# Convolution in the mixing stage: VectorE's own first tap first, the bank of diagonal products added last

## The chip, the cores and the metric

The kernel runs on one NeuronCore of a Trainium2 chip. The metric is device time in microseconds (us) of one execution, inputs and weights in HBM, result in HBM. The engines are named as in the profile: PE (TensorE matmul), PEld (its weight loads, which overlap), DVE (VectorE), ACT (ScalarE), POOL (GpSimd), SP (SyncE, here only a DMA queue).

## The reference

Two transformer blocks in a row on 256 tokens of 1024 channels. The first has two layers (l = 0, 1); layer 0 treats the tokens and a context of 256 more rows, layer 1 the tokens alone. A layer's mixing stage is one product with `w_in` and four mixers side by side, attention, a Fourier mixer, a convolution and a pooling mixer, each 256 channels wide:

```python
def conv_module(a, dw_w, dw_b, ln_g, ln_b, w_pw):
    glu = a[..., :W_CONV] * jax.nn.sigmoid(a[..., W_CONV:])
    y = lax.conv_general_dilated(glu, dw_w[:, None, :], window_strides=(1,),
        padding=[(CONV_WIDTH // 2, CONV_WIDTH // 2)], ...
        feature_group_count=W_CONV) + dw_b          # 31 taps, each channel by itself
    y = jax.nn.silu(layer_norm(y, ln_g, ln_b))
    return y @ w_pw
...
    mix = jnp.concatenate([attn, four, conv, pool], axis=-1) @ w_o
    x = x + gate1 * mix
    xn = rms_norm(x, g2) * (1 + scale2) + shift2
    return x + gate2 * swiglu(xn, w_fi, w_fo)
```

The gates, shifts and scales are products of a conditioning vector with `w_mod` (1024 x 6144 for each layer), one vector for the tokens and one for the context. The second block (dilated attention, a spatial gating unit, a gated feed-forward net) stands behind all this and is not touched.

## The kernel before

Channels lie on the 128 partitions, tokens along the free dimension: 512 columns in layer 0 (context and tokens), 256 in layer 1. fp32 precision comes from splitting each operand in a high and a low part and three matmuls (`mm3`, L273 to L275; L289 to L291 with tokens on the partitions). Weights arrive in halves of 128x1024 over SP's queue into `raw`; ACT casts the high part `wh` (L243), DVE subtracts the low part `wl` (L245), four buffers of each. A half is split when the one that held its buffers has been read for the last time.

In a mixing stage PE computes in this order: the convolution's inputs (`p_c`), q (`p_q`), k and v (`p_kv`), the Fourier input (`p_f`) and the pooling input (`p_p`). In between lie the works of the mixers. Each mixer is a generator that is spawned and runs in steps; a `yield` is the time it lets pass by a planner's clock, and `tick` moves that clock on for the matmuls. So the text is written in an interleaved order, and a scheduler with a timeline model of its own then sets the final order of instructions on PE, DVE, ACT and POOL; SP's queue keeps the written one.

The convolution works on two halves f = 0, 1 of 128 channels. `glu` (L636 on DVE) writes GP, the padded input. Of the 31 taps the first NPE = 8 are done by PE: `conv_diag` (on ACT, ahead) writes 8 diagonal matrices of the tap weights into a tile `cdg`, and `conv_pe` (L578) accumulates 8 fp32 matmuls of them with shifted views of GP in one PSUM bank `p_cv`. The trace has each of these as two records. The other 23 taps are DVE's in `conv_taps`: one instruction that copies bank plus bias into Y (L586), then 23 that add GP times a tap weight to Y (L588). Both halves run as `cv0` and `cv1` beside each other. The `cdg` tiles take two of the four buffers of tag `wm`, the `p_cv` banks two of four small PSUM buffers (`psm`) that the softmax scores `p_s` (L689), the transposes `p_qt` (L675) and the norms use too.

Behind both halves wait two things. `conv_ln` normalises Y (L604 to L620) and multiplies it with `w_pw` (`p_pw`, L627). In layer 0, `mod_bg` also starts then: for every 128 rows of a part of `w_mod`, POOL copies a column of `snap` (one column of the finished Y, L590) into a `wm` tile (L397), which orders the transfer behind it; the transfer of 512 KB is issued by ACT's queue (L398), and DVE forms two products with sums (L402 for the context, L404 for the tokens). Of each pair of tiles the layer's residual update (L891) needs the gate, and the next stage's first `nt` (L339) the norm's scale. `p_fy` is the Fourier mixer's second product, folded by DVE into U (L775, L776); `p_fa` (L755) its first; `p_pl` (L809) the pooling product, behind POOL's chain of sums S (L793 to L804) on the copied `p_p` (UP).

Of the kernel before, what the change touches and what calls it, by code (L numbers as in the profile page):

```python
# [28 lines left out]
OP = mybir.AluOpType  # L29
# [4 lines left out]
T = 256  # L34
NF = 22
EPS = 1e-6
TAPS = 31
# [10 lines left out]
NPE = 8  # L48
# [67 lines left out]
class Flow:  # L116
# [6 lines left out]
    def spawn(self, gen, delay=0.0):  # L123
        t = {"gen": gen, "done": False}
        self.n += 1
        heapq.heappush(self.q, (self.now + delay, self.n, t))
        return t
# [11 lines left out]
    def tick(self, c):  # L139
        self.now += c  # L140
        self._run()
# [13 lines left out]
def tile_kernel(ctx, tc, xin, pk_d, rows_d, lc_d, bc_d, wmod0, wmod, win, wout, wfi, wfo, wsm, win2, wproj, wout2,  # L155
                wgu, wdn, wst, pos, out, dump=None):
    nc = tc.nc
    V, S, G, PE, SP = nc.vector, nc.scalar, nc.gpsimd, nc.tensor, nc.sync
# [12 lines left out]
    def psm(name="psm"):  # L171
        return psum.tile([128, 512], F32, tag="sm", name=name)


    pk = cpool.tile([128, PK_W], F32, name="pk")
# [17 lines left out]
    def P(name, i=0, n=1):  # L193
        return pk[:, PK[name] + i:PK[name] + i + n]
# [40 lines left out]
    def split_to(i):  # L235
        while ld["split"] < min(i, len(halves)):
            j = ld["split"]
            dma_to(j + 1)
            n = halves[j][1]
            raw = ld["raw"].pop(j)  # L240
            h = ring.tile([128, 1024], F32R, tag="wh", name="wh", bufs=WB)
            lo = ring.tile([128, 1024], F32R, tag="wl", name="wl", bufs=WB)
            S.copy(h[:, :n], raw[:, :n])  # L243
            every = SPL.get(halves[j][2], 0) or (1 if j in SPH else 0)
            (G if every and j % every == 0 else V).tensor_tensor(lo[:, :n], raw[:, :n], h[:, :n].bitcast(F32),  # L245
                                                                 op=OP.subtract)
            ld["hl"][j] = (h, lo)
            ld["split"] += 1
            dma_to(j + 1 + RAW)
# [9 lines left out]
    def done(n, c, i=None):  # L259

        for j in (where[n, c] if i is None else [where[n, c][i]]):
            ld["done"].add(j)
        while ld["low"] in ld["done"]:
            ld["low"] += 1
        split_to(ld["low"] + WB)
# [254 lines left out]
    for l in range(2):  # L520
        streams = (0, 1) if l == 0 else (0,)
        ns = len(streams)
        N = 256 * ns
        cs = slice(0, N)
        with ExitStack() as mctx:
# [3 lines left out]
            GP = mp.tile([128, 2, ns, GW], F32, name="GP")  # L529
# [8 lines left out]
            Y = mp.tile([128, 2, N], F32, name="Y")  # L538
# [25 lines left out]
            cps = {}  # L564

            def conv_diag(f):

                w = lpool.tile([128, D], F32, tag="wm", name="cdg", bufs=WMB)
                for j in range(NPE):
                    S.activation(w[:, 128 * j:128 * j + 128], ident, AF.Copy,  # L570
                                 scale=pk[:, PK[f"dw_{l}"] + f * TAPS + j:PK[f"dw_{l}"] + f * TAPS + j + 1])
                return w

            def conv_pe(f, w):

                cps[f] = psm("p_cv")
                for j in range(NPE):
                    PE.matmul(cps[f][:, :N].rearrange("p (s t) -> p s t", t=T), w[:, 128 * j:128 * j + 128],  # L578
                              GP[:, f, :, j:j + T], start=j == 0, stop=j == NPE - 1)
                    tick(0.0017 * N)  # L580

            def conv_taps(f, delay):
                y = Y[:, f].rearrange("p (s t) -> p s t", t=T)
                dw = PK[f"dw_{l}"] + f * TAPS
                per = 0.35 * ns
                V.tensor_scalar(Y[:, f], cps[f][:, :N], P(f"db_{l}", f), None, op0=OP.add)  # L586
                for j in range(NPE, TAPS):
                    V.scalar_tensor_tensor(y, GP[:, f, :, j:j + T], pk[:, dw + j:dw + j + 1], y, op0=OP.mult, op1=OP.add)  # L588
                    yield per + delay
                G.tensor_copy(snap, Y[:, f, 0:1])  # L590
                pace[0] = snap

# [223 lines left out]
            cdg = [conv_diag(f) for f in range(2)]  # L816
# [8 lines left out]
            else:  # L825
                for f in range(2):
# [6 lines left out]
                            fm(ps4[2 + m][:, :N], n_, 1, 128 * m, cs)  # L833
                    glu(f, ps4[2 * f], ps4[2 * f + 1])
                    done(n_, f)
            for f in range(2):
                conv_pe(f, cdg[f])
            cv0 = spawn(conv_taps(0, CVD))
            cv1 = spawn(conv_taps(1, CVD), 0.5)
            cv = spawn(conv_ln(cv0, cv1))  # L840
            if l == 0:
# [10 lines left out]
            for s in ((1, 0) if l == 0 else (0, 1)):  # L852
# [6 lines left out]
                    S.copy(VT[:, 2 * (1 - s) + i], p[:, 128:256])  # L859
                preps[s] = spawn(qk_prep(s), 0.4)  # L860
            done(n_, 3)
            at = []
            if l == 0:
                at.append(spawn(attention(1, [preps[1]])))
# [77 lines left out]
        with ExitStack() as fctx:  # L942
# [64 lines left out]
            else:  # L1007
# [5 lines left out]
                for m in range(22):  # L1013
# [4 lines left out]
                    if m == 0:  # L1018
# [11 lines left out]
                                           op1=OP.mult)  # L1030
# [4 lines left out]
                for m in range(8):  # L1035
                    p = pmm("p_dn")
                    for part in range(2):
# [5 lines left out]
                                           op0=OP.mult, op1=OP.subtract)  # L1043
# [9 lines left out]
    with ExitStack() as bctx:  # L1053
# [238 lines left out]
        for c in range(4):  # L1292
            for b in range(2):
                m = 2 * c + b
                ps2 = []
                for hf in (1, 0):
                    p = pmm("p_pr")
                    for k in range(4):
# [11 lines left out]
                                       op1=OP.subtract)  # L1310
# [3 lines left out]
        for m in range(8):  # L1314
# [8 lines left out]
            elif m >= 4:  # L1323
# [5 lines left out]
                                   op0=OP.mult, op1=OP.subtract)  # L1329
# [5 lines left out]
    with ExitStack() as fctx:  # L1335
# [44 lines left out]
        for q, (m0, m1) in enumerate(OUT):  # L1380
            V.tensor_tensor(OT[:, m0:m1], OT[:, m0:m1], res[1][:, None, :].to_broadcast([128, m1 - m0, 256]),
                            op=OP.mult)
# [103 lines left out]
```

## Time and profile before

| | us |
|---|---|
| median of three runs | 1396.38 |
| the three runs | 1396.1, 1396.38, 1402.08 |
| profiled execution | 1395.62 |
| its span, first to last instruction | 1393.4 |
| PE busy in the span | 1339.7 (96%) |
| DVE busy | 932.3 (67%) |
| ACT busy | 617.5 (44%) |
| POOL busy | 287.9 (21%) |

The mean granted TensorE clock is 0.983 of full speed. The shares are averages over stages of different kinds: the feed-forward nets and the second block keep PE full; layer 0's mixing stage lies at about 60 to 262 us of the span and layer 1's at about 620 to 720 us. The tables of stretches, waits and instructions from which the prediction is made are in the section on rows below.

### The profile page before, as it was taken

What the parts mean: (1) busy time and instruction counts of PE and PEld (TensorE: products, weight loads), DVE (VectorE), ACT (ScalarE), POOL (GpSimd) and SP (SyncE); (2) the same over time, 40 slices, a digit from 0 to 9 for tenths busy, and PEclk for the clock granted to TensorE, in tenths of its full rate; (3) what the DMA queues carried; (4) which work ended last, traced back from release to release, by engine and by line L of the source; (5) the groups of instructions that cost most, each with busy time, mean ns of one, the idle gap of its engine ahead of it and who ended that gap; (6) DMA issues with size and microseconds to landing.
All of it is one profiled execution on the core that took longest, in us unless ns stands there. A gap on an engine that the chain in (4) does not pass through costs nothing.

```text
span 1393.4 us, 23072 instructions
## 1 busy us (share of the span) xinstructions
PE 1339.7 (96%) x9000; PEld 1193.2 (86%) x9000; DVE 932.3 (67%) x1597; ACT 617.5 (44%) x1030; POOL 287.9 (21%) x302
## 2 busy tenths in 40 slices
PE   6799889999999999999899999999999999999997
PEld 2578558888888888889689999999899999999997
DVE  4969999899885333349757666666665567755553
ACT  5623452523214232334555554455665444544452
POOL 3524535233340000121520000120100002322211
PEclk9799989999999999999999999999999999999998
DMA  8322443477895222343225555665325335555463
GB/s 321 136 92 79 166 154 134 152 272 232 278 323 179 91 91 63 104 137 107 78 83 189 183 182 156 187 242 191 122 98 175 122 125 179 181 182 181 153 196 106
DMA packets 66477, 223.77 MB, mean 161 GB/s; under 512 B 7488, under 2 KB 8640, under 8 KB 66368
## 3 DMA queue, kind: packets, MB, share of 16 engines
q1 hardware_dynamic: 53824, 178.16, 38.3%
q10 hardware_dynamic: 12080, 42.50, 9.0%
q0 software_dynamic: 464, 1.64, 0.3%
q8 instruction: 70, 1.15, 0.3%
q14 instruction: 39, 0.32, 0.1%
HBM read 221.22 MB, written 1.05 MB: 160 GB/s over the span
## 4 chain that ended last, share of the span: by engine, by line
PE 84%; DVE 9%; issue 2%; DMA 2%; POOL 1%; ACT 1%; SPq 0%; DVEq 0%; POOLq 0%; ACTq 0%
PE p_dn L273 6%; PE p_dn L275 6%; PE p_dn L274 6%; PE p_ua L273 4%; PE p_ua L274 4%; PE p_ug L273 4%; PE p_ug L275 4%; PE p_ug L274 4%; PE p_ua L275 4%; DVE wm L404 2%; DVE jg L402 2%; PE p_bq L289 2%; PE p_bq L290 2%; PE p_bq L291 2%; PE p_ga L275 2%
## 5 line engine op out<-in xcount | busy, mean ns | idle before, releaser
L245 DVE TENSOR_TENSOR wl<-raw,wh 128x1024 fp32r<-128x1024 f32 (+2 forms) x340 | 390.5, 1151 | 277.7 <-ACT wh L243 275.7
L243 ACT CAST wh<-raw 128x1024 fp32r<-128x1024 f32 (+1 forms) x344 | 331.6, 972 | 310.0 <-PE p_ug L274 89.2
L275 PE MATMUL p_dn<-HH,wl 128*128 128x256 f32 (+1 forms) x550 | 171.9, 313 | 0.5 <-DVE wl L245 0.5
L273 PE MATMUL p_dn<-HH,wh 128*128 128x256 f32 (+1 forms) x550 | 172.0, 313 | 0.0
L274 PE MATMUL p_dn<-HL,wh 128*128 128x256 f32 (+1 forms) x550 | 171.9, 312 | 0.0
L315 POOL TENSOR_TENSOR ss<-ss,sq 128x256 f32<-128x256 f32 (+1 forms) x43 | 49.8, 1158 | 422.2 <-ACT sq L314 284.7
L273 PE MATMUL p_ug<-AH,wh 128*128 128x258 f32 (+2 forms) x368 | 121.9, 332 | 0.6 <-DVE XC L891 0.6
L273 PE MATMUL p_ua<-AH,wh 128*128 128x258 f32 (+2 forms) x368 | 122.0, 333 | 0.4 <-ACT usg L950 0.3
L275 PE MATMUL p_ug<-AH,wl 128*128 128x258 f32 (+2 forms) x368 | 122.0, 332 | 0.0
L274 PE MATMUL p_ug<-AL,wh 128*128 128x258 f32 (+2 forms) x368 | 121.9, 331 | 0.0
L274 PE MATMUL p_ua<-AL,wh 128*128 128x258 f32 (+2 forms) x368 | 121.9, 331 | 0.0
L275 PE MATMUL p_ua<-AH,wl 128*128 128x258 f32 (+2 forms) x368 | 121.7, 331 | 0.0
L275 PEld LDWEIGHTS p_dn<-HH,wl 128*128 128x128 f32 x550 | 104.4, 190 | 6.7 <-DVE wl L245 0.7
L273 PEld LDWEIGHTS p_dn<-HH,wh 128*128 128x128 f32 x550 | 104.4, 190 | 6.1 <-ACT wh L243 0.2
L274 PEld LDWEIGHTS p_dn<-HL,wh 128*128 128x128 f32 x550 | 104.4, 190 | 6.1
L404 DVE SCALAR_TENSOR_TENSOR wm<-wm,scb 128x1024 f32<-128x1024 f32 x80 | 100.9, 1265 | 11.2 <-DMA wm<-in_wmod 10.4
L273 PEld LDWEIGHTS p_ug<-AH,wh 128*128 128x128 f32 x368 | 69.3, 188 | 8.1 <-DVE XC L891 0.8
L273 PEld LDWEIGHTS p_ua<-AH,wh 128*128 128x128 f32 x368 | 69.2, 188 | 7.7 <-ACT usg L950 0.5
L274 PEld LDWEIGHTS p_ua<-AL,wh 128*128 128x128 f32 x368 | 69.4, 189 | 7.3 <-DVE AL L341 0.2
L275 PEld LDWEIGHTS p_ua<-AH,wl 128*128 128x128 f32 x368 | 69.4, 189 | 7.1
L274 PEld LDWEIGHTS p_ug<-AL,wh 128*128 128x128 f32 x368 | 69.5, 189 | 6.9
L275 PEld LDWEIGHTS p_ug<-AH,wl 128*128 128x128 f32 x368 | 69.4, 189 | 6.9
(375 smaller groups left out, 3415.5 us busy)
## 6 DMA issues: line engine op xcount, KB each, us to landing
raw<-in_wfi SPq DMA_DIRECT2D x88, 512.0 KB, 4.0
raw<-in_win SPq DMA_DIRECT2D x84, 512.0 KB, 4.0
wm<-in_wmod ACTq DMA_DIRECT2D x80, 512.0 KB, 4.4
raw<-in_wgu SPq DMA_DIRECT2D x44, 512.0 KB, 3.8
raw<-in_wout SPq DMA_DIRECT2D x24, 512.0 KB, 3.6
raw<-in_wfo SPq DMA_DIRECT2D x32, 384.0 KB, 3.1
raw<-in_wfo SPq DMA_DIRECT2D x32, 320.0 KB, 3.3
raw<-in_wdn SPq DMA_DIRECT2D x16, 384.0 KB, 3.1
```

The lines of the kernel that those rows point to most:

```text
L243: S.copy(h[:, :n], raw[:, :n])
L245: (G if every and j % every == 0 else V).tensor_tensor(lo[:, :n], raw[:, :n], h[:, :n].bitcast(F32), op=OP.subtract)
L273: PE.matmul(ps, w[0], a[0], start=first, stop=False, **kw)
L274: PE.matmul(ps, w[0], a[1], start=False, stop=False, **kw)
L275: PE.matmul(ps, w[1], a[0], start=False, stop=last, **kw)
L289: PE.matmul(ps, a[0], w[0], start=k == 0, stop=False)
L290: PE.matmul(ps, a[0], w[1], start=False, stop=False)
L291: PE.matmul(ps, a[1], w[0], start=False, stop=k == KT - 1)
L315: (eng or G).tensor_tensor(ss[0][:, cs], ss[0][:, cs], sq[:, :n], op=OP.add)
L402: V.scalar_tensor_tensor(jg, w, 1.0, scb[:, 1], op0=OP.mult, op1=OP.mult, accum_out=modv[:, l, part, 1, k:k + 1])
L404: V.scalar_tensor_tensor(w, w, 1.0, scb[:, 0], op0=OP.mult, op1=OP.mult, accum_out=modv[:, l, part, 0, k:k + 1])
```

## The change

`conv_taps` no longer begins with the bank. The first instruction multiplies GP by DVE's first tap weight and adds the bias (L586, a tensor_scalar from SBUF), 22 taps follow (L590 of the new text), then the generator waits until the bank exists and adds it (L594). `conv_pe` for both halves moves from ahead of `cv0` to behind `done(n_, 3)`, the end of k and v in the written text. Lines behind the loop have numbers larger by 6 in the new text (L590 `snap` becomes L596, `glu` L642).

```diff
--- before.py
+++ after.py
@@ -583,10 +583,16 @@
                 y = Y[:, f].rearrange("p (s t) -> p s t", t=T)
                 dw = PK[f"dw_{l}"] + f * TAPS
                 per = 0.35 * ns
-                V.tensor_scalar(Y[:, f], cps[f][:, :N], P(f"db_{l}", f), None, op0=OP.add)
-                for j in range(NPE, TAPS):
+                V.tensor_scalar(y, GP[:, f, :, NPE:NPE + T], pk[:, dw + NPE:dw + NPE + 1], P(f"db_{l}", f), op0=OP.mult,
+                                op1=OP.add)
+                yield per + delay
+                for j in range(NPE + 1, TAPS):
                     V.scalar_tensor_tensor(y, GP[:, f, :, j:j + T], pk[:, dw + j:dw + j + 1], y, op0=OP.mult, op1=OP.add)
                     yield per + delay
+                while f not in cps:
+                    yield 0.3
+                V.tensor_tensor(Y[:, f], cps[f][:, :N], Y[:, f], op=OP.add)
+                yield per
                 G.tensor_copy(snap, Y[:, f, 0:1])
                 pace[0] = snap
 
@@ -833,8 +839,6 @@
                             fm(ps4[2 + m][:, :N], n_, 1, 128 * m, cs)
                     glu(f, ps4[2 * f], ps4[2 * f + 1])
                     done(n_, f)
-            for f in range(2):
-                conv_pe(f, cdg[f])
             cv0 = spawn(conv_taps(0, CVD))
             cv1 = spawn(conv_taps(1, CVD), 0.5)
             cv = spawn(conv_ln(cv0, cv1))
@@ -859,6 +863,8 @@
                     S.copy(VT[:, 2 * (1 - s) + i], p[:, 128:256])
                 preps[s] = spawn(qk_prep(s), 0.4)
             done(n_, 3)
+            for f in range(2):
+                conv_pe(f, cdg[f])
             at = []
             if l == 0:
                 at.append(spawn(attention(1, [preps[1]])))
```

Where the scheduler puts the instructions can be read from the built programs. PE, layer 0, around q: the two banks as they stood (-), between matmuls of q.

```order
 L290 MATMUL p_q<-wl,AH 128x256
 L291 MATMUL p_q<-wh,AL 128x256
-L578 MATMUL p_cv<-GP,cdg 128x512 x8
 L289 MATMUL p_q<-wh,AH 128x256
 L290 MATMUL p_q<-wl,AH 128x256
 L291 MATMUL p_q<-wh,AL 128x256
-L578 MATMUL p_cv<-GP,cdg 128x512 x8
 L289 MATMUL p_q<-wh,AH 128x256
```

Both are gone from there. PE, layer 0, at the end of `p_f`: the first bank as it stands now (+). The `p_qt` are transposes of the context's q and k.

```order
 L275 MATMUL p_f<-AH,wl 128x512
 L273 MATMUL p_f<-AH,wh 128x512
+L681 MATMUL p_qt<-ident,qt_781 128x128 x3
+L578 MATMUL p_cv<-GP,cdg 128x512
+L681 MATMUL p_qt<-ident,qt_815 128x128 x3
+L578 MATMUL p_cv<-GP,cdg 128x512 x7
 L274 MATMUL p_f<-AL,wh 128x512
-L675 MATMUL p_qt<-ident,qt_801 128x128 x3
-L675 MATMUL p_qt<-ident,qt_835 128x128 x3
 L275 MATMUL p_f<-AH,wl 128x512
 L273 MATMUL p_p<-AH,wh 128x512
```

The first bank is behind q, k, v and nearly all of `p_f`. PE further on, in the changed program: the second bank, behind the first 24 matmuls of `p_p`; `qt_866` and `qt_895` are the tokens' q and k, `p_s` the scores.

```order
+L274 MATMUL p_p<-AL,wh 128x512
+L275 MATMUL p_p<-AH,wl 128x512
+L681 MATMUL p_qt<-ident,qt_866 128x128 x3
+L578 MATMUL p_cv<-GP,cdg 128x512 x8
+L681 MATMUL p_qt<-ident,qt_895 128x128 x3
+L695 MATMUL p_s<-KTt,QT_493 128x256 x4
```

The scores stand directly behind the second bank. DVE, layer 0, in the changed program: the last taps, the two adds of the banks and what follows up to the first modulation products.

```order
L673 TENSOR_TENSOR qt_895<-qt_895,qt_896 128x256
L590 SCALAR_TENSOR_TENSOR Y<-GP,pk,Y 128x512 x2
L594 TENSOR_TENSOR Y<-p_cv,Y 128x512
L673 TENSOR_TENSOR qt_895<-qt_895,qt_903 128x128
L590 SCALAR_TENSOR_TENSOR Y<-GP,pk,Y 128x512
L676 TENSOR_TENSOR qt_895<-qt_895,rs_r 128x384
L594 TENSOR_TENSOR Y<-p_cv,Y 128x512
L698 TENSOR_REDUCE ast<-p_s 128x1 x4
L730 RECIPROCAL asum<-asum 128x2
L402 SCALAR_TENSOR_TENSOR jg,modv<-wm,scb 128x1024
```

The minima of the scores (L698) are behind the last add. POOL at the same place: the `snap` copies of the two halves, the sums S of the pooling mixer's first half, and the copies into `wm`.

```order
+L596 COPY snap<-Y 128x1
+L799 TENSOR_TENSOR S_482<-UP 128x2x271
+L801 TENSOR_TENSOR S_483<-S_482 64x2x269
+L808 TENSOR_TENSOR S_482<-S_482,lc 64x2x256
+L808 TENSOR_TENSOR S_482<-S_483,lc 64x2x256
+L810 TENSOR_TENSOR S_482<-S_482,UP 128x2x256
+L596 COPY snap<-Y 128x1
+L397 COPY wm<-snap 128x1 x9
```

Before, the chain S lay among the q and k products of POOL and its last step behind the second `snap`. In layer 1 the banks move from `p_q` into `p_p` in the same manner.

## Rows read from the trace of the kernel before

**Rows 1.** Table of stretches: window and length, each engine's busy us, clock, DMA.

```profile
core 0: us, PE busy (x) PEld busy (x) DVE busy (x) ACT busy (x) POOL busy (x), PEclk, DMA share, GB/s
78.00:93.00 15.00, 15.00 (x44) 7.29 (x44) 7.57 (x11) 0.37 (x1) 0.00 (x0) 1.00 0.17 60
148.00:222.00 74.00, 66.43 (x311) 42.75 (x311) 69.46 (x131) 31.97 (x81) 34.29 (x35) 0.88 0.51 163
262.00:612.00 350.00, 349.73 (x1605) 289.06 (x1604) 211.38 (x319) 105.55 (x150) 62.29 (x82) 1.00 0.53 178
673.00:684.00 11.00, 6.19 (x25) 4.19 (x25) 9.42 (x17) 4.01 (x10) 8.74 (x11) 0.84 0.28 95
```

**Rows 2.** Waits of DVE, 78 to 250 us: us in total, times, longest.

```profile
DVE Y L586 <- PE p_cv L578: 7.0, 1, 7.0
DVE wl L245 <- ACT wh L243: 2.5, 3, 0.9
```

**Rows 3.** Timeline of DVE, layer 0: start, duration, instruction, idle before.

```profile
77.87 0.68 DVE L636 SCALAR_TENSOR_TENSOR GP<-sg,p_c 128x512 f32<-128x512 f32 x1
85.51 0.75 DVE L586 TENSOR_SCALAR Y<-p_cv,pk 128x512 f32<-128x512 f32 x1 [6.95 <-PE p_cv L578]
86.37 6.26 DVE L588 SCALAR_TENSOR_TENSOR Y<-GP,pk,Y 128x512 f32<-128x512 f32 x8
...
139.11 1.68 DVE L588 SCALAR_TENSOR_TENSOR Y<-GP,pk,Y 128x512 f32<-128x512 f32 x1
...
148.45 1.89 DVE L402 SCALAR_TENSOR_TENSOR jg<-wm,scb 128x1024 f32<-128x1024 f32 x1 [2.17 <-DMA wm<-in_wmod]
...
247.32 0.85 DVE L339 SCALAR_TENSOR_TENSOR nt<-XC,modv,p_rb 128x256 f32<-128x256 f32 x2
```

**Rows 4.** Timeline of POOL, and the chain of waits: start, duration.

```profile
143.65 0.86 POOL L397 COPY wm<-snap 128x1 f32<-128x1 f32 x4
...
144.19 4.15 DMA wm<-in_wmod
```

**Rows 5.** Timeline of PE, layer 0.

```profile
78.43 7.04 PE L578 MATMUL p_cv<-GP,cdg 128*128 128x512 f32 x16
...
122.82 0.39 PE L274 MATMUL p_f<-AL,wh 128*128 128x512 f32 x1
123.05 0.82 PE L675 MATMUL p_qt<-ident,qt 128*128 128x128 f32 x6
...
130.45 0.70 PE L689 MATMUL p_s<-KTt,QT 64*128 64x256 f32 x4
```

**Rows 6.** DVE's groups by shape, 78 to 145 and 126 to 250 us: count, busy, mean ns, idle.

```profile
L586 DVE TENSOR_SCALAR Y<-p_cv,pk 128x512 f32<-128x512 f32 x2 | 1.5, 751 | 7.1 <-PE p_cv L578 7.0
...
L588 DVE SCALAR_TENSOR_TENSOR Y<-GP,pk,Y 128x512 f32<-128x512 f32 x8 | 8.7, 1082 | 0.0
...
L667 DVE TENSOR_TENSOR qt<-qt,qt 128x256 f32<-128x256 f32 x2 | 1.9, 958 | 0.0
...
L604 DVE TENSOR_TENSOR Y<-Y,p_mean 128x512 f32<-128x512 f32 x2 | 1.3, 676 | 0.0
```

**Rows 7.** One line's durations (minimum, median, maximum): a tensor_scalar from SBUF.

```profile
L1374 DVE TENSOR_SCALAR OT<-XC,pk x1: 352/352/352, 1384.3 to 1384.3; 128x256 f32<-128x256 f32 x1
```

**Rows 8.** PE's groups by shape, 78 to 148 us.

```profile
L755 PE MATMUL p_fa<-lc,U 128*128 128x256 f32 x16 | 4.5, 386 | 0.0
L768 PE MATMUL p_fy<-lc,fa 128*128 128x129 f32 x18 | 3.0, 286 | 0.0
```

**Rows 9.** Waits of PE, 126 to 250 us.

```profile
PE p_pw L627 <- ACT Y L620: 2.5, 1, 2.5
PE p_s L689 <- DVE awo L737: 2.2, 1, 2.2
```

**Rows 10.** Waits of PE, layer 1, 634 to 718 us.

```profile
PE p_qt L675 <- DVE qt L670: 2.7, 1, 2.7
PE p_fw L783 <- DVE U L776: 2.1, 1, 2.1
```

## The prediction

> **What bounds the kernel now.** I read the table of stretches first, to see which engine is full where. From 262 to 612 us TensorE (PE) is busy 349.7 of 350 us at the full clock [rows 1]; the change touches nothing there, so that stretch can only move as a whole. What the change can alter lies in the two mixing stages: about 75 to 250 us in layer 0 and 630 to 720 us in layer 1.
>
> In layer 0 the limit changes hands. From 78 to 93 us PE is busy all 15 us while VectorE (DVE) works 7.57 of them. From 148 to 222 us DVE is busy 69.46 of 74 us, and PE 66.43 of 74 at a mean granted clock of 0.88, part of the time at the lower of its two levels (1.2 instead of 2.4 GHz) [rows 1]. In the second stretch DVE works through the modulation products (L402, L404), and the layer can't end before it is through. In layer 1 PE is the fuller engine again, but from 673 to 684 us it works only 6.19 of 11 us [rows 1].
>
> The waits say why. DVE's largest before the products is 7.0 us, once, on p_cv [rows 2]. In its timeline the second GP begins at 77.87 and lasts 0.68 us, then 6.95 us are idle, and the first tap instruction begins at 85.51; the last tap ends at 139.11 + 1.68, or 140.8. The first modulation product begins at 148.45 and the first `nt` of the next stage at 247.32 [rows 3]. Between tap and product stands a chain: snap, POOL's copies into the `wm` tiles, a transfer of 4.15 us [rows 4].
>
> **The change part by part, layer 0.** *The early start.* DVE's first tap now needs GP alone, so the 7.0 us on p_cv go [rows 2, 3]. What stands behind them on DVE (46 taps, four weight splits, the q and k work) moves up as far as its inputs allow. Those come from q, k, v and f, which PE now reaches earlier by the two moved banks: 7.04 us busy for one [rows 5], some 6.9 from its start to where PE is through, 13.8 for both. So inputs come up by more than DVE does, and little of the 7.0 is lost to them; two weight splits that wait 0.8 us each for the cast before p_f's end (part of 2.5 us in three) [rows 2] should wait as long again, on the cast or on k's squares.
>
> *The exchanged instructions.* The count stays at 24 for a half. The bias add that reads the bank took 0.751 us [rows 6]. The new first tap reads SBUF; the nearest row is a tensor_scalar of half its width from SBUF at 0.352 us [rows 7], so it lies between 0.35 and 0.75, and I take 0.6 because twice the half-width row is 0.70. The last add reads bank and Y in one tensor_tensor of the same shape as L604, 0.676 us [rows 6], where a tap of 6.26/8 = 0.78 us [rows 3] falls away. That is a gain of 0.25 for a half, 0.5 for both (bounds 0 to 1).
>
> *Less neighbourly taps.* The last 8 taps took 1.082 us each and two q products 0.958 us [rows 6], beside POOL's chain of sums; the first 8 took 0.78 [rows 3]. Eight times 0.30 plus two times about 0.5 is 3.4 us. In the new order POOL's chain follows the first snap and so stands behind most taps; I take 3.2 (0 to 3.4).
>
> DVE would thus reach its last add at 140.8 - 7.0 - 0.5 - 3.2, about 130.
>
> *The bank that it then needs.* The order puts the first bank behind 46 of the 48 matmuls of p_f's second half, the second behind half of p_p. PE reaches the 47th of these at 122.82 now [rows 5], so at 109.0 without the banks. Add the first bank 6.9, six transposes 0.8 [rows 5], the rest of p_f 0.5, 24 matmuls of p_p at 0.23 us from start to start (the distance of the two p_f and p_qt rows) 5.5, four Fourier matmuls of 4.5/16 = 0.28 us [rows 8] 1.1, three transposes 0.4 and the second bank 6.9: ready at about 131.1. It comes some 1 us behind DVE (0 to 4), and the last add ends near 132, 8.5 us before the last tap did. That is the place where the gain is capped: not DVE's taps but PE's second bank ends last.
>
> *What hangs on the last add.* POOL's second snap stands behind a chain of sums that needs the first half of p_p, copied out some 6 us before the second bank is ready. The chain's rows of before sum to about the same 6 to 7 us, so the snap is late by 0 to 2 us. From snap to first product it is then POOL's copies (0.86 for four) and 4.15 us of transfer [rows 4], with a small remainder: about 137.5 for the first product instead of 148.45, or 11 us earlier. The ACT queue issues this transfer now ahead of the table load for the softmax; the wait for the snap therefore also holds the first exponentials, which themselves need p_s, and p_s stands behind the same bank, so I cost it at nothing; without that cover it is at most the 0 to 2 us above.
>
> *What is left of it at the layer's end.* The order moves 1.6 us of DVE work (a split, four Fourier folds, less one update) from ahead of the first product to behind it. By DVE alone the `nt` at 247.32 [rows 3] comes 11 - 1.6, or 9 us earlier. PE says less. When the first product starts, PE has more left than before: 24 matmuls of p_p (5.5), the remaining Fourier products (3.0 of p_fy for 18, some 1.7 of p_fa [rows 8]), 10 us in all. From 148 to 222 it loses 74 - 66.4 = 7.6 us idle and 0.12 x 74 = 8.9 us to the clock [rows 1]. If it loses just as much afterwards, PE ends only 0 to 2 us earlier. If the work that was left fills these gaps, it ends earlier by up to the 9 to 11 of DVE. The gaps that I expect to shrink are the 2.5 us for the normalised convolution at L627, which is ordered far earlier now, and part of the 2.2 us of p_s behind the attention's DVE steps [rows 9]. A half of the way from the one to the other: **5 us** for layer 0 (0 to 11).
>
> The Trainium skill ("TensorE: Matmul & The Clock Gate", on how the clock's oscillation bites in real kernels) says that a PE that starves for its inputs drops to the lower clock and pays for the gap again. The 0.88 of the stretch with the gaps, against 1.00 where PE is full, agrees [rows 1]. By that rule each gap that closes here would give back more than its own length, and each that opens at the first softmax, which now has no p_p matmuls under it, would cost more.
>
> **Layer 1.** Here the banks have half the columns. q, k, v come up by the two banks' 6.9 us of PE, and DVE's taps start without waiting for the banks. PE itself does the same work, so what can be gained is its idle time behind DVE: 2.7 us on qt, 2.1 us on the Fourier fold U [rows 10]. DVE reaches both with a lead of a few microseconds; against it the banks hold two of the four small PSUM buffers until the last adds, and the scores that now stand ahead of the Fourier products need such buffers. I take 3 of the 4.8 (0 to 7, the upper end with the lost clock of 0.84 x 11 us [rows 1] given back).
>
> **Sum.** 5 + 3 = 8 us. The profiled execution took 1395.62 us, of which 1393.4 are its span; 1395.6 - 8 = 1387.6. The median of the three runs is 0.8 above it, so the forecast is **1388 us**.
>
> **The rivals.** *A, PE's gaps close.* DVE's 9 to 11 us arrive whole and the clock stays up: 11 in layer 0, 5 to 7 in layer 1, 1378 to 1380 us. For it: DVE is at 94% in 148 to 222 us. Against it: PE is near its own limit, as counted.
>
> *B, PE is bound throughout.* The early start only lets DVE wait later, for the second bank, and the 10 us of matmuls shifted behind the softmax cost what they gain: 0 to 2 in layer 0 and 2 to 3 in layer 1, 1392 to 1395. For it: PE's count; the first softmax steps lie bare on PE. Against it: 7.6 us of idle PE in which DVE was what it waited for.
>
> *C, slower.* The attention is the chain that sets the end. Its first p_s stands at 130.45 now [rows 5] and would stand behind the second bank at 131.5 at best; it then waits on DVE, whose minima for the softmax stand behind the last add. If the taps keep their stretch of 3.2 and DVE's inputs give back half of the 7.0, the last add comes at 137 and the softmax 6 us later than now; PE, in order, stands before its own p_p with it. Layer 1, where the scores wait for the buffers that the banks hold, adds some 2: 1396.4 + 6 + 2, about 1404. It decides if the last add ends later than about 135.
>
> *D, not as described.* The products are to stand behind q, k and v. In the order they stand farther back, behind p_f and half of p_p. That is in the sum above; had they stood right behind v, the second bank would have been ready near 112 and the cap would be DVE's 130, which is 1 to 2 us better (1386).
>
> **How the numbers follow.** The forecast's own case (1383 to 1391) has a chance of 0.45, A 0.14, B 0.26, C 0.12, D's better value 0.03. Half a percent, 7 us, is about what a measurement of this kernel can tell from no change: faster means under 1389.4, slower over 1403.4. About 0.32 of the forecast's 0.45 lies under 1389.4, with A and D 0.49; B with the other 0.13 of the forecast gives 0.39 within 0.5%; C, just over the bound by its price, is counted as slower, 0.12. For 8 in 10 the range runs from 1379, most of A, to 1400, all of B and the mildest form of C.
>
> **What would show it.** In the changed profile DVE's first tap should follow the first GP at about 77 to 78 us without a wait; a wait on p_cv of 0 to 4 us should stand at the last add near 131; the first modulation product should begin near 137.5 and `nt` between 236 and 247. If the first product comes by 138 and `nt` still near 246, B is right, and PE's waits between 132 and 150 will show the softmax. If the last add comes after 135, C. In layer 1 the waits on qt and U should fall below 2 us together. The forecast is wrong if PE shows new waits over 5 us in 130 to 150, or a lower clock in a stretch that had 1.00.

## The result, and the profile after

The changed kernel takes 1383.43 us (median of four runs, 1382.44 to 1385.46) against 1398.66 us for the kernel before, run beside it (four runs, 1396.1 to 1402.08). The ratio is 0.9891, 95% interval 0.9863 to 0.992: faster by 11 to 19 us, where 8 were forecast. The profiled execution took 1382.44 us and its span is 1380.7, 12.7 less than the span before.

The page of the profile after has the same 9000 matmuls in it, in less time:

```profile
span 1380.7 us, 23081 instructions
...
PE 1336.6 (97%) x9000; PEld 1190.3 (86%) x9000; DVE 921.3 (67%) x1597; ACT 616.5 (45%) x1030; POOL 284.6 (21%) x302
...
PE 89%; DVE 6%; issue 2%; ACT 1%; POOL 1%; DMA 1%; SPq 0%; DVEq 0%; POOLq 0%; ACTq 0%
```

The last line is the chain that ended last: PE holds 89% of it now, DVE 6%; before, they held 84% and 9%.

DVE's timeline in layer 0 (start, duration, instruction, idle before) answers to [rows 3]:

```profile
78.15 0.54 DVE L586 TENSOR_SCALAR Y<-GP,pk 128x512 f32<-128x512 f32 x1
...
123.02 1.47 DVE L590 SCALAR_TENSOR_TENSOR Y<-GP,pk,Y 128x512 f32<-128x512 f32 x2
...
125.87 1.44 DVE L676 TENSOR_TENSOR qt<-qt,rs_r 128x384 f32<-128x384 f32 x1
132.09 0.69 DVE L594 TENSOR_TENSOR Y<-p_cv,Y 128x512 f32<-128x512 f32 x1 [4.78 <-PE p_cv L578]
...
136.95 1.23 DVE L402 SCALAR_TENSOR_TENSOR jg<-wm,scb 128x1024 f32<-128x1024 f32 x1 [0.76 <-DMA wm<-in_wmod]
...
237.49 0.87 DVE L339 SCALAR_TENSOR_TENSOR nt<-XC,modv,p_rb 128x256 f32<-128x256 f32 x2
```

The first tap follows GP without a wait, the only wait on a bank (4.78 us) stands at the last add, the first modulation product is 11.5 us earlier and the first `nt` 9.8 us earlier than in [rows 3].

PE's timeline at the same place, for [rows 5]:

```profile
125.01 7.04 PE L578 MATMUL p_cv<-GP,cdg 128*128 128x512 f32 x16
131.89 0.49 PE L681 MATMUL p_qt<-ident,qt 128*128 128x128 f32 x3
132.31 1.40 PE L695 MATMUL p_s<-KTt,QT 64*128 64x256 f32 x8
135.59 0.89 PE L705 MATMUL p_s<-ident,pe 128*128 128x128 f32 x4 [1.88 <-ACT pe L701]
```

The first scores come 1.9 us later than before, but four of them at once (eight records) instead of two. The stretches for [rows 1] (window and length, busy us of PE, PEld, DVE, ACT, POOL, then PE's clock):

```profile
148.00:222.00 74.00, 71.17 (x372) 47.94 (x371) 71.54 (x133) 33.15 (x77) 35.14 (x34) 0.98 0.47 158
```

PE idles 2.8 us there instead of 7.6, and the clock is 0.98 instead of 0.88. A part of that is paid for just ahead of it, where PE now waits 1.88 us at the first softmax step; from 130 to 150 us, before and after:

```profile
130.00:150.00 20.00, 18.81 (x104) 13.12 (x102) 15.63 (x23) 11.80 (x31) 14.46 (x18) 1.00 0.30 102
130.00:150.00 20.00, 17.95 (x86) 10.62 (x85) 14.84 (x31) 10.98 (x32) 5.19 (x10) 0.91 0.50 172
```

PE's waits in layer 1, the whole of what is listed from 632 us to the end of its mixing stage (to 718 us), for [rows 10]:

```profile
PE p_s L695 <- DVE Y L594: 1.2, 1, 1.2
PE p_s L705 <- ACT pe L701: 0.2, 1, 0.2
PE p_o L734 <- ACT pT L707: 0.2, 1, 0.2
```

The waits on qt and U are gone, a small one for the buffers that the banks hold has come.

**Where the 12.7 us came from.** PE runs the feed-forward net of layer 0 in both kernels with next to no gaps (from 300 to 612 us it is busy all 312 us in either), so the matmuls behind it date the end of layer 0. I take the last matmul of `p_c` in layer 1 for that and the first of `p_bq` in the second block for the end of layer 1. One line of each tile's view gives them (count, shortest, median and longest ns, first and last start), before and after:

```profile
L273 PE MATMUL p_c<-AH,wh x64: 277/388/795, 36.8 to 633.8; 128*128 128x512 f32 x32, 128*128 128x256 f32 x32
L289 PE MATMUL p_bq<-wh,AH x192: 274/281/392, 921.3 to 1071.4; 128*128 128x256 f32 x192
```

```profile
L273 PE MATMUL p_c<-AH,wh x64: 276/388/796, 37.0 to 628.0; 128*128 128x512 f32 x32, 128*128 128x256 f32 x32
L289 PE MATMUL p_bq<-wh,AH x192: 274/281/393, 908.6 to 1058.8; 128*128 128x256 f32 x192
```

Layer 0 ends 633.8 - 628.0 = 5.8 us earlier, layer 1 takes 280.6 instead of 287.5 us from there, 6.9 less. The sum is 12.7; behind that nothing changes.

PE's own row in the table of stretches splits this gain. The stretches are layer 0 from the first matmul of q, and layer 1, before and then after:

```profile
75.50:633.80 558.30, 545.42 (x2775) 443.42 (x2776) 395.45 (x638) 190.88 (x334) 145.05 (x169) 0.98 0.47 158
633.80:921.30 287.50, 279.29 (x2242) 268.79 (x2241) 202.00 (x368) 148.54 (x248) 41.61 (x44) 0.99 0.47 151
```

```profile
75.80:628.00 552.20, 542.38 (x2776) 440.28 (x2777) 388.61 (x639) 190.88 (x334) 141.66 (x169) 0.99 0.47 160
628.00:908.60 280.60, 278.93 (x2241) 268.98 (x2240) 198.03 (x368) 147.34 (x248) 42.57 (x44) 0.99 0.47 155
```

In layer 0, PE's idle time falls from 12.9 to 9.8 us, and its busy time for the same matmuls by 3.0, which goes with the higher clock of 148 to 222 us; the two make 6.1, because q begins 0.3 us later. In layer 1 nearly all of the gain is idle time, 8.2 us before and 1.7 after.

### The profile page after: what moved, and what is told of

It is laid out like the page before. It is cut to its first block, busy times and chain, and to the rows that moved or that the text cites. A ratio compares the mean times of both kernels' runs of the same rounds, so it can differ in the third digit from the quotient of the medians.

```text
span 1380.7 us, 23081 instructions
## 1 busy us (share of the span) xinstructions
PE 1336.6 (97%) x9000; PEld 1190.3 (86%) x9000; DVE 921.3 (67%) x1597; ACT 616.5 (45%) x1030; POOL 284.6 (21%) x302
## 4 chain that ended last, share of the span: by engine, by line
PE 89%; DVE 6%; issue 2%; ACT 1%; POOL 1%; DMA 1%; SPq 0%; DVEq 0%; POOLq 0%; ACTq 0%
PE p_dn L273 6%; PE p_dn L275 6%; PE p_dn L274 6%; PE p_ua L273 4%; PE p_ua L274 4%; PE p_ug L274 4%; PE p_ua L275 4%; PE p_ug L275 4%; PE p_ug L273 4%; PE p_wo L273 2%; PE p_wo L274 2%; PE p_wo L275 2%; PE p_bq L289 2%; PE p_bq L290 2%; PE p_bq L291 2%; PE p_ga L275 2%
## 5 line engine op out<-in xcount | busy, mean ns | idle before, releaser
L245 DVE TENSOR_TENSOR wl<-raw,wh 128x1024 fp32r<-128x1024 f32 (+2 forms) x340 | 390.0, 1149 | 280.6 <-ACT wh L243 280.0
L404 DVE SCALAR_TENSOR_TENSOR wm<-wm,scb 128x1024 f32<-128x1024 f32 x80 | 99.9, 1252 | 12.0 <-DMA wm<-in_wmod 11.3
```

The source lines that it names most:

```text
L404: V.scalar_tensor_tensor(w, w, 1.0, scb[:, 0], op0=OP.mult, op1=OP.mult, accum_out=modv[:, l, part, 0, k:k + 1])
```

## The experiments

The theory to begin with was the prediction's: DVE's early start makes the gain, in layer 0 because the modulation products start earlier, and the late second bank only caps it. The rival was that PE's new order carries it.

**early_only**: the first tap as in the change, the banks where they stood.

```diff
+            for f in range(2):
+                conv_pe(f, cdg[f])
             cv0 = spawn(conv_taps(0, CVD))
...
             done(n_, 3)
-            for f in range(2):
-                conv_pe(f, cdg[f])
```

> DVE begins with its own tap and adds the bank last, but PE computes both banks where they stood, ahead of q. Theory (the gain is DVE's early start; in the changed kernel the second bank behind half of p_p is what caps it, DVE idles 4.8 us for it): the taps run under the banks, no wait of DVE on p_cv, the first modulation product comes before 130 us in layer 0 (136.95 in the changed kernel), and the time is 1378 to 1386, as fast as the changed kernel or up to 4 us faster. Rival (the gain is PE's new order: q, k and v 13.8 us earlier): q, k and v stay where they were, and the time is 1392 to 1399, near the kernel before.

It took 1407.84 us, ratio 1.0064 (1.0042 to 1.0086): slower than before. Neither had expected that. DVE did what the theory says, and more of it, in its timeline:

```profile
115.67 0.69 DVE L594 TENSOR_TENSOR Y<-p_cv,Y 128x512 f32<-128x512 f32 x1
...
122.22 1.23 DVE L402 SCALAR_TENSOR_TENSOR jg<-wm,scb 128x1024 f32<-128x1024 f32 x1 [1.20 <-DMA wm<-in_wmod]
...
141.52 1.61 DVE L676 TENSOR_TENSOR qt<-qt,rs_r 128x384 f32<-128x384 f32 x1
...
155.37 0.82 DVE L676 TENSOR_TENSOR qt<-qt,rs_r 128x384 f32<-128x384 f32 x1
```

The taps are done at 116 us and the first product begins at 122, 26 us earlier than before and 15 earlier than in the changed kernel; yet the layer ends later than in both. The last line says why: the tokens' second q and k part (L676) is through DVE only at 156 us, in the kernel before at 144 and in the changed one at 127. The products, 1.2 to 2.3 us each, now stand between the q and k steps on DVE. PE has the price, in the table of stretches:

```profile
126.00:148.00 22.00, 18.19 (x98) 14.01 (x96) 21.60 (x37) 9.24 (x20) 19.45 (x17) 1.00 0.48 160
148.00:222.00 74.00, 59.73 (x276) 35.15 (x276) 69.32 (x130) 31.68 (x83) 31.68 (x34) 0.86 0.41 136
```

That is 3.8 and 14.3 us idle, where the kernel before had 1.1 in the first stretch (20.89 busy of 22) and 7.6 in the second [rows 1], with DVE as full as before: a full DVE is not the same as a DVE that does what is waited for.

**move_only**: the banks behind q, k and v, and DVE begins with the bank as before, once its last product is in.

```diff
-                cps[f] = psm("p_cv")
+                bank = psm("p_cv")
...
+                cps[f] = bank
...
+                while f not in cps:
+                    yield 0.3
                 V.tensor_scalar(Y[:, f], cps[f][:, :N], P(f"db_{l}", f), None, op0=OP.add)
                 for j in range(NPE, TAPS):
```

> The banks stand behind q, k and v as in the changed kernel, but DVE begins with the finished bank as before. Theory (early start): the taps can't start before about 117 us instead of 85.5, DVE has little to do from 78 to 117, the first modulation product comes some 15 to 20 us later than the 148.45 of before, 1404 to 1415. Rival (PE's order carries the gain): 1383 to 1390.

1407.35 us, ratio 1.0064 (1.004 to 1.0088). The theory's direction and size, with the first product at 168.85 us. So in these two schedules neither half of the change brings anything alone; each costs 8 us.

**layer0_only** and **layer1_only**: the whole change in one layer, the old text in the other.

```diff
+            conv_taps = conv_taps_new if l == 0 else conv_taps_old
...
+            if l != 0:
+                for f in range(2):
+                    conv_pe(f, cdg[f])
             cv0 = spawn(conv_taps(0, CVD))
...
             done(n_, 3)
+            if l == 0:
+                for f in range(2):
+                    conv_pe(f, cdg[f])
```

> The whole change in layer 0 alone; layer 1 as before. Theory (the two layers gain by themselves, as the distance between the two traces says: 5.9 us at the first matmul of the down projection of layer 0): 5 to 7 us under the kernel before. Rival (the layers are coupled, for instance through the transfers and products of the modulation that run on into layer 0's feed-forward net): under 3 us or over 9.

> The whole change in layer 1 alone; layer 0 as before. Theory: 6 to 8 us under the kernel before, PE's waits on qt (2.7 us), on the Fourier fold U (2.1) and on the normalised convolution (2.0) gone as in the changed kernel. Rival (layer 1's gain needs layer 0's): under 4 us.

1393.61 us, ratio 0.996 (0.9943 to 0.9976), for layer 0, and 1389.62, ratio 0.9946 (0.9921 to 0.997), for layer 1; the product of the ratios is 0.9906, within the interval of the whole change. The layers gain by themselves, by these ratios 5.6 and 7.6 us at a median of 1399.55.

**early_hold**: a second theory after early_only. As early_only, but in layer 0 the column that POOL copies into the `wm` tiles, and so what releases their transfers, is one of the tokens' finished q.

```diff
+                def mod_hold():
+                    yield from wait(cv0, cv1)
+                    while len(preps) < 2:
+                        yield 0.3
+                    yield from wait(*preps.values())
+                    pace[0] = QT[0][:, 1, 255:256]
+                    yield from mod_bg([(0, 2, True, BG0),
...
```

> As early_only (DVE's own tap first, banks ahead of q), but in layer 0 the copies that release the transfers of the modulation weights read the last column of the tokens' transposed q instead of the convolution's column, so that the modulation products stand on DVE behind all q and k work. New theory after early_only came out slow at 1407.8 us: DVE's products at 122 us (before: 148) stood in front of the q and k steps on DVE, and PE, in order, waited with them (18 us idle from 126 to 222 us instead of 8.7). Then the hold takes most of that away: 1396 to 1402, near the kernel before, since PE's order of q, k, v is also that of before. Rival (the products in front of q and k aren't the cause, the early adds or the changed order of POOL are): 1404 to 1410, as early_only.

1391.0 us, ratio 0.995 (0.9935 to 0.9965). The hold is worth 17 us, more than expected, and the kernel is faster than before although PE computes q, k and v as late as before. Its first product begins at 142.62 us, 20 later than in early_only, and its layer 0 ends at 625.3 us, the earliest so far:

```profile
L273 PE MATMUL p_c<-AH,wh x64: 276/392/796, 37.7 to 625.3; 128*128 128x512 f32 x32, 128*128 128x256 f32 x32
```

PE's rows of layer 0 say where the time was, in early_only and then in early_hold: 23.0 us idle in the one, 7.9 in the other, with nearly the same busy time.

```profile
74.00:641.60 567.60, 544.65 (x2769) 441.70 (x2770) 390.23 (x635) 188.61 (x330) 138.43 (x169) 0.98 0.46 156
75.10:625.30 550.20, 542.28 (x2770) 441.15 (x2771) 387.50 (x635) 189.45 (x330) 141.92 (x169) 0.99 0.48 161
```

**bank_after_q**: the changed kernel with the banks between q and k, v.

```diff
             done(n_, 2)
+            for f in range(2):
+                conv_pe(f, cdg[f])
...
             done(n_, 3)
-            for f in range(2):
-                conv_pe(f, cdg[f])
```

> As the changed kernel, but the banks stand behind q and ahead of k and v. New theory (the banks are filler for PE: behind k and v they fill the time in which PE waits for the steps from k to the first scores, and DVE's last add behind the second bank keeps the modulation products out of q and k's way): k comes as late as in the kernel before and the products come in front of q and k as in early_only, so 1398 to 1410. Rival, the prediction's (the second bank behind half of p_p only caps DVE, 4.8 us): 1378 to 1384.

1407.37 us, ratio 1.0073 (1.0051 to 1.0094). First product at 124.9 us, as slow as early_only. The prediction's view of the second bank as a mere cap falls here: with the bank early, DVE is free early, and fills the time with products in front of q and k. The late bank keeps the products behind them; early_hold shows that it is not the only way to do that.

**npe6** and **npe4**: the changed kernel with 6 and 4 taps on PE, the rest on DVE (`-NPE = 8`, `+NPE = 6` or `4`).

> The changed kernel with 6 instead of 8 taps on PE and 25 instead of 23 on DVE. PE's work falls by 2/8 of both layers' banks, 5.2 us; DVE gets four more taps of 0.7 us in layer 0 (2.8) where it waits 4.8 us for the second bank, and four of 0.4 in layer 1. If PE's work sets the end (its idle from 100 to 262 us is 4.7 us): 1377 to 1381. If the filler is what counts, PE waits instead: 1383 to 1386. If DVE sets it: 1384 to 1388.

> 4 taps on PE, 27 on DVE: PE's work falls by 10.4 us, DVE gets eight taps of 0.7 us (5.6) in layer 0 and eight of 0.4 (3.2) in layer 1, more than the 4.8 us that it waits. If PE's work sets the end: 1373 to 1379. If DVE's last add sets it, it comes some 2 us later than 132: 1382 to 1388.

1395.4 us, ratio 0.9971 (0.9952 to 0.9989), and 1396.7, ratio 0.999 (0.9979 to 1.0001): slower than the changed kernel by 12 and 13 us, over every expectation, though PE has 5 and 10 us less to do. This is no clean test of the amount of work: with shorter banks the scheduler put both in a row behind `p_f` and set the scores and products behind them in another order. In npe6 one place shows what that costs. PE issues two scores (four records) at 149.18; DVE's timeline from there, and PE's:

```profile
148.93 2.06 DVE L404 SCALAR_TENSOR_TENSOR wm<-wm,scb 128x1024 f32<-128x1024 f32 x1
...
150.93 2.28 DVE L402 SCALAR_TENSOR_TENSOR jg<-wm,scb 128x1024 f32<-128x1024 f32 x1
...
153.14 0.41 DVE L698 TENSOR_REDUCE ast<-p_s 128x1 f32<-128x256 f32 x1
```

```profile
149.18 1.80 PE L695 MATMUL p_s<-KTt,QT 64*128 64x256 f32 x4
155.55 1.31 PE L705 MATMUL p_s<-ident,pe 128*128 128x128 f32 x4 [4.57 <-ACT pe L701]
```

The minimum of the scores (0.41 us) waits for two products in front of it on DVE, the exponential for the minimum, PE for the exponential: 4.57 us. The granted clock of the stretch that follows is down to 0.60 (table of stretches):

```profile
155.00:161.00 6.00, 5.45 (x19) 2.58 (x19) 6.00 (x11) 2.66 (x11) 4.43 (x4) 0.60 0.39 115
```

**combo**: layer 0 as in early_hold, layer 1 as in the change (each by `if l == 0` and `if l == 1` around the two places of `conv_pe`).

> Layer 0 as in early_hold (banks ahead of q, DVE's own tap first, modulation products released only behind the q and k work), layer 1 as in the changed kernel. Theory (the layers gain by themselves; layer 0 of early_hold ended 2.7 us earlier than the changed kernel's, by the last matmul of p_c in layer 1, 625.3 against 628.0 us; layer 1 of early_hold took 289.5 us from there to the second block, the changed one 280.6): 1379 to 1383 us. Rival (a small edit moves the schedule by as much as the whole gain, and layer 0 of early_hold was luck): 1386 to 1395.

1383.56 us, ratio 0.9898 (0.9864 to 0.9932); in its profile 1380.44. The two ways to a good layer 0 are equal within what can be measured.

**after_hold**: the changed kernel with the hold of early_hold.

> The changed kernel with the modulation products released by the tokens' transposed q instead of the convolution's column. Theory: the second bank already keeps them behind the q and k work there, so nothing changes: 1381 to 1386. Rival (the products, not the bank's place, are what layer 0 hangs on, and a hold helps here too): 1372 to 1378.

1385.28 us, ratio 0.9911 (0.9882 to 0.9941). The hold changes nothing where the late bank already does its work.

**after_cvd06** and **after_cvd12**: the changed kernel with another planner's wait between two taps (`-CVD, FOD = 0.9, 1`, `+CVD, FOD = 0.6, 1` or `1.2, 1`).

> The changed kernel with the planner's wait between two taps cut from 0.9 to 0.6 us; no instruction is added or taken away, the banks stay in their places in PE's order, the scores and products behind them are interleaved a little differently. If the gain is the place of the banks and DVE's early start: 1380 to 1388. If it is the particular interleaving behind them: 1390 or more.

> As after_cvd06, with 1.2 us: the first scores stand some rows farther behind the second bank on PE. If the gain is the place of the banks and DVE's early start: 1380 to 1388. If it is the particular interleaving behind them: 1390 or more.

1394.05 us, ratio 0.9972 (0.9953 to 0.9991), and 1398.39, ratio 1.0002 (0.9976 to 1.0027). Banks and early start are in both, and about three quarters to all of the gain are gone. So the two together don't make the gain: the particular interleaving behind them decides whether it comes. In after_cvd12 about half of the loss is idle time of PE, 14.3 us in layer 0 and 4.8 in layer 1 (9.8 and 1.7 in the changed kernel). In after_cvd06 layer 0 keeps most of its gain (554.5 us against 552.2, table below) and layer 1 loses all of it, to the clock rather than to idle time. Its layer 1 behind the last add:

```profile
671.70:677.70 6.00, 4.02 (x14) 2.63 (x14) 3.54 (x8) 4.74 (x11) 3.61 (x3) 0.80 0.52 162
677.70:683.70 6.00, 6.00 (x29) 3.82 (x29) 0.86 (x2) 3.53 (x11) 0.00 (x0) 0.50 0.04 15
683.70:689.70 6.00, 6.00 (x29) 5.65 (x31) 1.71 (x7) 2.02 (x7) 3.78 (x6) 0.56 0.00 0
```

and the same stretch behind the last add of the changed kernel:

```profile
670.00:676.00 6.00, 4.81 (x13) 3.19 (x13) 4.99 (x12) 4.03 (x9) 5.79 (x6) 0.73 0.44 147
676.00:682.00 6.00, 5.51 (x40) 3.70 (x38) 2.01 (x7) 4.16 (x12) 2.90 (x4) 0.98 0.08 30
682.00:688.00 6.00, 6.00 (x48) 4.53 (x46) 2.32 (x7) 3.38 (x10) 0.00 (x0) 1.00 0.00 0
```

PE counts as busy in both, but at 0.50 and 0.56 of full speed (the lower level, 1.2 GHz) for 12 us in the one, and at 0.98 and 1.00 in the other. By the timelines the changed kernel has `p_fw` (the Fourier mixer's product of U, 3.47 us in a row) between the scores and the softmax's transposes there, and the other only `p_mean` with a wait in it.

**What all runs have in common.** Times are distances in the profiles: from the first matmul of q to the last of `p_c` (layer 0), from there to `p_bq` (layer 1), and from the first of q to the last attention result in layer 0, the last `AL<-awo` (L741, in the changed kernels L747 or a near line).

| kernel | median us | layer 0 | layer 1 | q to last attention result | from there to the end of layer 0 |
|---|---|---|---|---|---|
| before | 1398.66 | 558.3 | 287.5 | 141.6 | 416.7 |
| layer1_only (layer 0 as before) | 1389.62 | 562.4 | 279.7 | 145.6 | 416.8 |
| changed | 1383.43 | 552.2 | 280.6 | 137.4 | 414.8 |
| layer0_only | 1393.61 | 554.9 | 289.6 | 137.0 | 417.9 |
| after_hold | 1385.28 | 555.3 | 280.7 | 137.1 | 418.2 |
| combo | 1383.56 | 550.6 | 280.9 | 133.3 | 417.3 |
| early_hold | 1391.0 | 550.2 | 289.5 | 133.1 | 417.1 |
| npe4 | 1396.7 | 554.6 | 292.8 | 136.6 | 418.0 |
| after_cvd06 | 1394.05 | 554.5 | 287.8 | 136.8 | 417.7 |
| npe6 | 1395.4 | 559.0 | 285.6 | 142.0 | 417.0 |
| after_cvd12 | 1398.39 | 560.8 | 286.5 | 145.8 | 415.0 |
| early_only | 1407.84 | 567.6 | 288.1 | 148.0 | 419.6 |
| bank_after_q | 1407.37 | 570.1 | 285.4 | 154.8 | 415.3 |
| move_only | 1407.35 | 568.1 | 289.9 | 123.6 | 444.5 |

In 13 of 14 kernels layer 0 ends 414.8 to 419.6 us behind the last attention result. PE is nearly full there, busy 412.5 of the 416.7 us before and 409.5 of 414.8 after. So what these kernels gain or lose in layer 0 lies ahead of that result; the constant distance alone doesn't show that it is the attention which holds PE up. Only in move_only, where the convolution is 20 us late, something else is last: the modulation products. Three lines of its timelines, from POOL, ACT and PE, give the chain from the last product of a part to the next stage's first matmul:

```profile
255.39 1.47 POOL L409 TENSOR_TENSOR modv<-modv,pk 128x8 f32<-128x8 f32 x2 [0.67 <-DVE jg L402]
256.89 0.91 ACT L340 ACTIVATE AH<-nt,modv 128x256 fp32r<-128x256 f32 x2 [6.97 <-POOL modv L409]
257.45 0.58 PE L273 MATMUL p_ua<-AH,wh 128*128 128x256 f32 x1 [1.99 <-ACT AH L340]
```

So late products can end the layer, as the prediction read it. In layer 1 the distance from the last attention result to `p_bq` is 206.6 us in the kernel before and in the changed one alike. From these lines (the last attention result of layer 0, before and after):

```profile
217.07 0.29 DVE L741 TENSOR_TENSOR AL<-awo,AH 128x128 fp32r<-128x128 f32 x1
```

```profile
213.15 0.28 DVE L747 TENSOR_TENSOR AL<-awo,AH 128x128 fp32r<-128x128 f32 x1
```

The changed kernel has the tokens' q and k ready 16.7 us earlier (142.58 to 125.87), the first attention result (`awo`) 11.4 earlier (153.69 to 142.28), the last 3.9 earlier. Most of the early start is lost again on the way, and PE's row from the first to the last result, before and after, says on what:

```profile
153.69:217.07 63.38, 57.71 (x262) 35.98 (x263) 59.32 (x115) 29.14 (x72) 29.80 (x31) 0.87 0.47 150
142.28:213.15 70.87, 68.31 (x349) 44.51 (x347) 68.41 (x133) 33.78 (x82) 35.13 (x35) 0.99 0.50 170
```

PE is busy 10.6 us longer there, with 349 matmul records instead of 262, about the 10 us of matmuls that the prediction counted as left over. It does them with fewer gaps at a higher clock. The chain that ended last agrees: from 110 to 270 us it spends 33% of its time on DVE's two product lines (L402, L404) before and 8% in the changed kernel, where PE's matmuls have most of it.

The same program differs from profile to profile as well: layer 0 is the same in before and layer1_only, and took 558.3 and 562.4 us. Differences under some 4 us of one layer between two profiles say nothing; the medians decide there.

## Why the prediction was right, and where it was not

*The steps on DVE.* They came as worked out: first tap at 78.15 us without a wait (77 to 78), the SBUF tensor_scalar 0.54 (taken 0.6), the last add 0.69 (0.676), taps at the end 0.735 each with POOL's chain behind them (0.78 instead of 1.08), the last add at 132.09 (131), the first product at 136.95 (137.5), `nt` at 237.49 (236 to 247, 9 earlier by DVE alone). DVE arrived at its last add at 127.3, some 3 us earlier than summed, and waited 4.8 us (0 to 4); the second bank ended last there, as said.

*Layer 0's total.* 5 us forecast, 5.8 measured in the profiles, 5.6 by layer0_only. I took the middle between PE's count (0 to 2) and DVE's early end (9 to 11), and no row stood behind a half: that the sum hit is in part luck. One way that I gave for it, work left over that fills PE's gaps, did come. Both gaps that I named, at L627 and at the scores behind L737 [rows 9], are gone from PE's waits. From 148 to 222 us the idle time fell by 4.8 us, and the loss to the clock, reckoned as in the prediction, is an estimated 1.5 us (0.02 x 74) instead of 8.9. Left out of the sum was what is given back elsewhere, from 130 to 150 us and in a new wait of 3.4 us on the next stage's first inputs (L341).

The other bound was the wrong step: that the layer's end moves up with the start of the modulation products. early_only started them 15 us earlier still and was 24 us slower than the change. What was missing is the rank of the products on DVE against the q and k steps that PE waits for.

*A sign against itself* that the prediction named did show: a lower clock in a stretch that had 1.00. It is 0.91 from 130 to 150 us, outweighed by the stretch behind it. The new wait there is 1.9 us, not over 5. It falls on the term that I put at nothing, the first exponentials behind the table load, which ACT begins only after a wait for POOL's copies:

```profile
133.67 1.28 ACT L701 ACT_TABLE_LOAD   x1 [0.72 <-POOL wm L397]
```

*Rival C* looked at the right place, the attention behind the second bank, and priced it with the wrong sign; its condition, a last add later than about 135 us, was not met (132.8). The first scores did come later, at 132.31 (131.5), but four together, where the kernel before had two at 130.45 and the others at 139.23 and 140.11. No tap and no product stood in their way any longer. *Rival A*, the closing gaps, has the right sign on PE, but of DVE's 9 to 11 us 9.8 arrived at `nt` and 5.8 at the layer's end; 1383.4 lies at the edge of the forecast's own case (1383 to 1391), above A's 1378 to 1380. *Rival B* counted PE's work rightly, but not the gaps that it filled. *Rival D's* number, banks right behind v for 1 to 2 us more, was not tried; bank_after_q, still farther ahead, cost 24.

*Layer 1's total* was the mis-sized term: 3 forecast (0 to 7), 6.9 measured. I counted the two waits on qt and U, 4.8 us, and took off some for the small buffers. Those cost 1.2 us; but a third wait of before went too, on the normalised convolution, and the waits fell from 8.2 to 1.6 us together:

```profile
PE p_pw L627 <- ACT Y L620: 2.0, 1, 2.0
```

`p_pw` stands just ahead of the attention's last product on PE in both kernels (at 710.41 and 697.88 us); its input is there in time now, and I had not followed the early convolution that far.

*The rule of the Trainium skill* ("TensorE: Matmul & The Clock Gate", on how the clock's oscillation bites) held in both directions: with most of the gaps of [rows 1] gone the clock of the stretch rose from 0.88 to 0.98, in the stretch with the new gap at the first softmax it fell from 1.00 to 0.91, and after_cvd06 lost its layer 1 to the lower level, 0.50 and 0.56 over 12 us behind a stretch in which PE was idle for 2.0 of 6 us.

*The 15 us of the medians* against 12.7 in the profiles: the profile of before was of one of its quicker executions (1395.62 at a median of 1398.66), which the forecast took for its base.

What stays open is how much of the gain would be left under another interleaving of the same text. The two tried with other planner's waits gave 1394 and 1398, after_hold 1385. The late banks are not needed as such: combo does as well with early banks in layer 0 and the hold. early_only, move_only and bank_after_q were each tried in one schedule only. How much of their loss belongs to the place of the banks, and how much to the interleaving, is not shown, except in early_only, where the hold alone gave 17 us back.

## What to carry to other kernels

An engine that works through background products at 95% need not be what bounds a stage. Split the time of the engine that carries the most work into idle and busy first; then look for the short steps that it waits for, and for what stands ahead of them in their queue. Starting background work earlier can cost more than starting it late: here 17 us lay in nothing but holding it behind q and k. And where a scheduler sets the order, repeat a change under a second planner's constant before calling its size a property of the idea.

## What the runs showed of the hardware

A DVE tensor_scalar from PSUM took longer here than one from SBUF that does a second operation on top. From PSUM it took 751 ns for 512 columns and 484 for 256, 1.04 ns a column; from SBUF 541 and 406 ns, 0.53 ns a column. L586 before and after:

```profile
L586 DVE TENSOR_SCALAR Y<-p_cv,pk x4: 484/618/751, 85.5 to 644.7; 128x512 f32<-128x512 f32 x2, 128x256 f32<-128x256 f32 x2
L586 DVE TENSOR_SCALAR Y<-GP,pk x4: 406/473/541, 78.2 to 634.3; 128x512 f32<-128x512 f32 x2, 128x256 f32<-128x256 f32 x2
```

Source and operations differ at once between the two, so that it is the source alone isn't shown.

And a PE that counts as busy all the time can stay at half its clock: 6.00 of 6.00 us at 0.50 in after_cvd06, behind a stretch with 2.0 us of idle time and with short matmuls of scores, transposes and sums in it.
